# FFN up-projections as 2x2 block products in seven multiplications, with the down-projections in a second phase

## The chip, the core and the metric

One core of a Trainium2 chip runs the program. The time is the device time of one execution in microseconds (us). The engines are PE (TensorE, the matmuls), DVE (VectorE), ACT (ScalarE), POOL (GpSimd) and SP (SyncE, which here only issues DMAs). Each runs its own instructions in order and waits on semaphores for the others.

## The reference

Two layers of a decoder trunk, batch 1, 1024 positions, 1024 channels, all in float32. Layer 0 is a retention layer, layer 1 differential attention over keys and values that are computed once; behind each stands the same kind of FFN, and the FFN is what changes here:

```python
D_FF = 2816                      # 22 blocks of 128
def conv_ffn(xn, w_up, conv_w, conv_b, w_down):
    h = xn @ w_up                # 1024 x 1024 times 1024 x 5632
    hp = jnp.pad(h, ((0, 0), (CONV_WIDTH - 1, 0), (0, 0)))
    hc = conv_b
    for j in range(CONV_WIDTH):  # 3 taps, causal, per channel
        hc = hc + hp[:, j:j + S] * conv_w[j]
    g, u = jnp.split(hc, 2, axis=-1)
    return (jax.nn.silu(g) * u) @ w_down
...
x = x + rms_norm(conv_ffn(rms_norm(x, ffn_norm_pre), ...), ffn_norm_post)
```

## The kernel before

Every large product is made from values split in two: a high part that TensorE takes as it is, and a low part that holds the rest. A product is then three matmuls (`mm3`, L96: high by high, high by low, low by high) that add up in one PSUM bank. The split of an operand (`split_to`, L81) is a copy on ACT for the high part and a subtraction on DVE for the low part.

Weights come through `load_w` (L85): a DMA from SP into one of two raw buffers (`rawp`, 1024 columns each, taken in turn in the order of the program), a multiplication by the norm's gain on POOL where there is one (L90), and the split into one of five `hl` buffers. A raw buffer is free for the next load when the low part is taken.

An FFN is run by `gated` (L479): the 22 blocks of 128 hidden channels go in eleven groups, one of 1, nine of 2 and one of 3. For each block `ffn_up` (L591) makes the gate block f and the up block 22 + f: for either, 2 halves of 512 positions x 8 k-blocks x 3 matmuls of 128x512 (`proj_t`). ACT and DVE run the convolution straight out of PSUM (L600, L604), ACT the Silu, POOL the product of the two (L611), and the split puts it into one of three `act` buffers. `down` (L501) multiplies a finished group by its rows of w_down: for each of 8 blocks of 128 positions, 6 matmuls per hidden block (L492) into one PSUM tile, which DVE adds to an accumulator in SBUF (L508, L510). The down products of group g are issued behind the first up block of group g + 1, so up and down products alternate on PE. PSUM is four tiles of two banks.

The norm ahead of the FFN is done by `finish` (L129), block by block of 128 positions, while PE runs the last products of the stage before: the scaled row block (ACT, L186) is transposed on PE (L120) and split into `xh`/`xl`. The first half of the first two up blocks is issued before the last of these blocks is through.

The order of instructions on an engine is set by the framework's scheduler from the order of the code, except where `manual_schedule` fixes it for named engines.

Of the kernel before, what the change touches and what calls it, by code (L numbers as in the profile page):

```python
# [12 lines left out]
F32 = mybir.dt.float32  # L13
F32R = mybir.dt.float32r
# [7 lines left out]
P = 128  # L22
# [28 lines left out]
def trunk(ctx: ExitStack, tc: tile.TileContext, A, out):  # L51
# [13 lines left out]
    gains4 = const.tile([P, 4, NK], F32, name="gains4")  # L65
# [30 lines left out]
    def mm3(out, sh, sl, mh, ml, start, stop):  # L96
        nc.tensor.matmul(out, sh, mh, start=start, stop=False)  # L97
        nc.tensor.matmul(out, sh, ml, start=False, stop=False)  # L98
        nc.tensor.matmul(out, sl, mh, start=False, stop=stop)  # L99
# [22 lines left out]

    def into_xt(ps, sb, xt):
        xh, xl = xt
        c, b = divmod(sb, 4)
        cols = slice(b * P, (b + 1) * P)
        split_to(xh[c][:, :, cols], xl[c][:, :, cols], ps)

    def finish(mm, add, pool, psp, gpost, x_old, x_new, xt, order=tuple(range(NS)), turn_first=False, late=()):  # L129
# [34 lines left out]
        for t in range(NS + 3):  # L164
# [3 lines left out]
            with tc.manual_schedule(engines=ORDERED):  # L168
# [15 lines left out]
                if c is not None:  # L184
                    xh = live["xh", c] = pool.tile([P, D], F32, name="xhn", tag="w4")
                    nc.scalar.activation(out=xh, in_=live.pop(("t", c)), func=AF.Copy, scale=live.pop(("q", c)))  # L186
# [77 lines left out]
    with ExitStack() as p1:  # L264
# [23 lines left out]
        with tc.tile_pool(name="p0", bufs=3, side="right") as p0:  # L288
# [37 lines left out]
            for i in range(2):  # L326
                nc.sync.dma_start(out=gains4[:, 2 + i, :], in_=A["ffn_norm_pre"][i])
# [151 lines left out]
    def gated(wk, up, n_blk, w_down, fin):  # L479
# [49 lines left out]
        rest = iter(())  # L529
        if isinstance(acts[-1], tuple):  # L530
            acts[-1], rest = acts[-1]
            next(rest)

        def mm(sb):
# [10 lines left out]
            if sb == 1:  # L545
                next(rest, None)
# [44 lines left out]
    def ffn_up(wk, layer, xt, tail, w_pool=None, late=None, on_drained=None):  # L591

        cw = []
        gpre = gains4[:, 2 + layer, :]

        def conv(n, ps, hc, c0, c1):
            if not cw:
                cw.append(wk.gp.tile([P, 2 * NF, 4], F32, name="cw"))
                nc.sync.dma_start(out=cw[0], in_=A["conv"][layer])
            nc.scalar.activation(out=hc[:, c0:c1], in_=ps[:, c0:c1], func=AF.Identity, scale=cw[0][:, n, 2:3],  # L600
                                 bias=cw[0][:, n, 3:4])
            for j in (1, 2):
                b = max(c0, j)
                nc.vector.scalar_tensor_tensor(out=hc[:, b:c1], in0=ps[:, b - j:c1 - j],  # L604
                                               scalar=cw[0][:, n, 2 - j:3 - j],
                                               in1=hc[:, b:c1], op0=ALU.mult, op1=ALU.add)

        def gate(hg, hu, act, c0, c1, eng):
            cs = slice(c0, c1)
            nc.scalar.activation(out=hg[:, cs], in_=hg[:, cs], func=AF.Silu)  # L610
            eng.tensor_tensor(out=hg[:, cs], in0=hg[:, cs], in1=hu[:, cs], op=ALU.mult)  # L611
            split_to(act[:, 0, cs], act[:, 1, cs], hg[:, cs])

        def tiles():
            return [wk.w4.tile([P, S], F32, name="hc", tag="w4") for _ in range(2)]

        def up(f):
            ns = (f, NF + f)
            if f == NF - 1:
                return up_last(ns)  # L620
            pss = []
            if f == 0:
                ws = []

                def load():
                    ws.extend(load_w(w_pool or wk.hlp, A["w_up"][layer, n], gpre) for n in ns)
                if late is None:
                    load()
                else:
                    late.append(load)  # L630
                for u in range(2):
                    next(tail)
                    pss.append(psp.tile([P, S], F32, name="ps"))
                    proj_t(pss[u], ws[u], xt, (0,))
                for _ in tail:
                    pass
                for ps, w in zip(pss, ws):
                    proj_t(ps, w, xt, (1,))
                if on_drained is not None:
                    on_drained()  # L640
            hc = tiles()
            for u, n in enumerate(ns):
                if f > 0:
                    w = load_w(wk.hlp, A["w_up"][layer, n], gpre)
                    pss.append(psp.tile([P, S], F32, name="ps"))
                    proj_t(pss[u], w, xt)
                conv(n, pss[u], hc[u], 0, S)
            act = wk.actp.tile([P, 2, S], F32R, name="act")
            gate(*hc, act, 0, S, nc.gpsimd)
            return act  # L650

        def up_last(ns):

            ws = [load_w(wk.hlp, A["w_up"][layer, n], gpre) for n in ns]
            hc = tiles()
            pss = [psp.tile([P, S], F32, name="ps") for _ in ns]
            for u, n in enumerate(ns):
                proj_t(pss[u], ws[u], xt, (0,))
                conv(n, pss[u], hc[u], 0, 512)
            act = wk.actp.tile([P, 2, S], F32R, name="act")  # L660
            gate(*hc, act, 0, 512, nc.vector)

            def rest():
# [502 lines left out]
```

## Time and profile before

| | us |
|---|---|
| median of 3 runs | 2941.19 (2940.98 to 2942.84) |
| the profiled execution | 2942.96 |
| its span, first to last instruction | 2941.2 |
| PE busy in the span | 2880.3 (98%) |
| DVE, ACT, POOL busy | 1469.9, 946.5, 668.4 |
| layer 0's FFN, about | 888 to 1600 |
| layer 1's FFN, about | 2180 to 2935 |

The page cuts the span into 40 equal slices and gives each engine's busy share in tenths; PEclk is the clock that TensorE was granted, in tenths of full speed. Matmuls overlap in the array, so the length of one matmul is not what it adds to the time: that is the distance from start to start. A row of waits names who waited, for whom, the total, how often and the longest.

### The profile page before, as it was taken

Reading aid. Unit: us, or ns where it says so; the run is one execution under the profiler, and the core shown is the slowest. Engines: PE = TensorE matmul, PEld = TensorE weight load, DVE = VectorE, ACT = ScalarE, POOL = GpSimd, SP = SyncE. Lnnn points to the kernel's source line nnn. Section 1 sums busy time; section 2 is a strip of 40 time slices with the busy share of each in tenths; the row PEclk is TensorE's granted clock in tenths of the full one; section 3 lists DMA queues with packets and bytes.
Section 4 is the critical chain, followed back from the end, with each engine's and each line's share of the span. In section 5 each row is a group of like instructions: output and inputs, shape, how many; then the busy total and the mean of one; then the engine's idle time right before and its main releaser. Section 6 shows DMA issues by size and latency. Waiting matters only on the chain. (4 is left out here: it accounts for less than half of the span.)

```text
span 2941.2 us, 35261 instructions
## 1 busy us (share of the span) xinstructions
PE 2880.3 (98%) x14452; PEld 2436.4 (83%) x14452; DVE 1469.9 (50%) x1722; ACT 946.5 (32%) x1462; POOL 668.4 (23%) x744
## 2 busy tenths in 40 slices
PE   8999999999999999999999999999999999999998
PEld 7898989888877888888888788888777888888886
DVE  4433433434446444444445687777554444444445
ACT  3323222211134222222224565555453222222222
POOL 1111120000033111211114334444332121121113
PEclk9999999999999999999999999999999999999999
DMA  4111111321232111111113332233252111111112
GB/s 141 53 54 51 51 52 37 121 79 59 78 122 86 51 50 43 51 50 51 43 44 120 118 80 75 68 85 93 73 204 80 43 50 51 47 47 44 58 58 100
DMA packets 86225, 210.45 MB, mean 72 GB/s; under 512 B 9648, under 2 KB 35248, under 8 KB 86064
## 3 DMA queue, kind: packets, MB, share of 16 engines
q1 hardware_dynamic: 62432, 180.67, 19.3%
q10 hardware_dynamic: 23632, 27.53, 2.9%
q8 instruction: 114, 1.87, 0.3%
q14 instruction: 47, 0.39, 0.0%
HBM read 164.12 MB, written 31.46 MB: 66 GB/s over the span
## 5 line engine op out<-in xcount | busy, mean ns | idle before, releaser
L97 PE MATMUL ps<-xh,hl 128*128 128x512 f32 x1952 | 764.3, 392 | 3.7 <-DVE xl L83 2.4
L99 PE MATMUL ps<-xh,hl 128*128 128x512 f32 x1952 | 762.3, 391 | 0.0
L98 PE MATMUL ps<-xl,hl 128*128 128x512 f32 x1952 | 760.0, 389 | 0.5 <-DVE xl L83 0.5
L492 PE MATMUL ps<-hl,act 128*128 128x512 f32 x2880 | 664.5, 391 | 1.1 <-DVE acc L508 1.1
L492 PEld LDWEIGHTS ps<-hl,act 128*128 128x128 f32 x2880 | 540.8, 188 | 114.3 <-DVE acc L508 1.9
L604 DVE SCALAR_TENSOR_TENSOR hc<-ps,cw,hc 128x1023 f32<-128x1023 f32 (+4 forms) x184 | 226.6, 1232 | 536.8 <-ACT hc L600 536.5
L90 POOL TENSOR_TENSOR raw<-raw,gains 128x1024 f32<-128x1024 f32 x120 | 238.0, 1984 | 1124.3 <-DMA raw<-in_w_up 1032.7
L99 PEld LDWEIGHTS ps<-xh,hl 128*128 128x128 f32 x1952 | 366.9, 188 | 79.7
L97 PEld LDWEIGHTS ps<-xh,hl 128*128 128x128 f32 x1952 | 367.0, 188 | 79.6 <-DVE xl L83 2.6
L98 PEld LDWEIGHTS ps<-xl,hl 128*128 128x128 f32 x1952 | 366.8, 188 | 78.8 <-DVE xl L83 1.0
L82 ACT ACTIVATE hl<-raw 128x1024 fp32r<-128x1024 f32 x228 | 240.0, 1054 | 500.3 <-PE ps L492 320.0
L83 DVE TENSOR_TENSOR hl<-raw,hl 128x1024 fp32r<-128x1024 f32 x228 | 289.9, 1272 | 114.2 <-ACT hl L82 114.0
L510 DVE TENSOR_TENSOR acc<-ps,acc 128x1024 f32<-128x1024 f32 x192 | 234.6, 1222 | 148.4 <-PE ps L492 147.1
L600 ACT ACTIVATE hc<-ps,cw 128x1024 f32<-128x1024 f32 (+1 forms) x92 | 107.6, 1170 | 485.1 <-PE ps L99 475.7
L611 POOL TENSOR_TENSOR hc<-hc 128x1024 f32<-128x1024 f32 x42 | 100.8, 2400 | 346.8 <-DVE hc L604 319.9
L97 PE MATMUL ps<-hl,xh 128*128 128x256 f32 x544 | 154.9, 286 | 1.7 <-ACT xh L82 1.7
L99 PE MATMUL ps<-hl,xl 128*128 128x256 f32 x544 | 155.3, 286 | 0.8 <-DVE xl L83 0.7
L98 PE MATMUL ps<-hl,xh 128*128 128x256 f32 x544 | 154.8, 285 | 0.0
L853 ACT ACTIVATE s<-s,m 128x256 f32<-128x256 f32 (+7 forms) x128 | 99.1, 775 | 102.1 <-POOL m L852 101.7
L82 ACT ACTIVATE act<-hc 128x1024 fp32r<-128x1024 f32 (+1 forms) x46 | 47.1, 1024 | 239.9 <-POOL hc L611 231.1
L97 PEld LDWEIGHTS ps<-hl,xh 128*128 128x128 f32 x544 | 105.2, 194 | 2.8 <-ACT xh L82 2.6
L99 PEld LDWEIGHTS ps<-hl,xl 128*128 128x128 f32 x544 | 105.3, 194 | 1.6 <-DVE xl L83 1.5
(188 smaller groups left out, 3701.1 us busy)
## 6 DMA issues: line engine op xcount, KB each, us to landing
raw<-in_w_up SPq DMA_DIRECT2D x88, 512.0 KB, 3.5
raw<-in_w_down SPq DMA_DIRECT2D x44, 512.0 KB, 3.5
raw<-in_w_t SPq DMA_DIRECT2D x32, 512.0 KB, 3.5
xold<-x SPq DMA_DIRECT2D x24, 512.0 KB, 4.6
raw<-in_w_v SPq DMA_DIRECT2D x16, 512.0 KB, 3.5
oret<-t ACTq DMA_DIRECT2D x32, 256.0 KB, 2.3
raw<-in_a_w_out SPq DMA_DIRECT2D x16, 512.0 KB, 3.6
on<-oret SPq DMA_DIRECT2D x16, 512.0 KB, 4.6
```

The costliest lines, as they stand in the source:

```text
L82: nc.scalar.activation(out=hi, in_=src, func=AF.Copy)
L83: nc.vector.tensor_tensor(out=lo, in0=src, in1=hi.bitcast(F32), op=ALU.subtract)
L90: nc.gpsimd.tensor_tensor(out=v, in0=v, in1=gain.unsqueeze(2).broadcast_to([P, gain.shape[1], n]), op=ALU.mult)
L97: nc.tensor.matmul(out, sh, mh, start=start, stop=False)
L98: nc.tensor.matmul(out, sh, ml, start=False, stop=False)
L99: nc.tensor.matmul(out, sl, mh, start=False, stop=stop)
L492: nc.tensor.matmul(ps[:, half, :], a, ws[f][:, m, hs], start=f == 0 and n == 0, stop=f == len(ws) - 1 and n == 2)
L510: nc.vector.tensor_tensor(out=acc[sb], in0=flat(ps), in1=acc[sb], op=ALU.add)
L600: nc.scalar.activation(out=hc[:, c0:c1], in_=ps[:, c0:c1], func=AF.Identity, scale=cw[0][:, n, 2:3], bias=cw[0][:, n, 3:4])
L604: nc.vector.scalar_tensor_tensor(out=hc[:, b:c1], in0=ps[:, b - j:c1 - j], scalar=cw[0][:, n, 2 - j:3 - j], in1=hc[:, b:c1], op0=ALU.mult, ...
L611: eng.tensor_tensor(out=hg[:, cs], in0=hg[:, cs], in1=hu[:, cs], op=ALU.mult)
L853: nc.scalar.activation(out=s[:, :w], in_=s[:, :w], func=AF.Exp, scale=0.125, bias=m, accum_out=l[:, c:c + 1])
```

## The change

**The product.** For a pair (gate block f, up block 22 + f) the weights are a 2x2 block matrix, 2 blocks of output channels (gate, up) by 2 halves of K (512 channels each), and the normed input another, 2 halves of K by 2 halves of the positions. The four output blocks are made from seven block products instead of eight (Winograd's form), each of 128 x 512 x 512, that is 4 k-blocks x 3 matmuls of 128x512. The seven operands of the input side are x11, x21 (first half of the positions, as before) and t2, t3, t1, t4, x22, sums and differences of quarters, made once per layer and split; the seven of the weight side are made for each pair: a11, s2, a21', s1, a12, a22, a12', with four additions on POOL and seven splits of 512 columns (`weights`, `split_part`). Five additions on DVE (`plus`) put the four output blocks together out of PSUM, in SBUF. The convolution then reads SBUF.

**The input.** `Staged` takes the place of `new_xt`: the second half of the positions is kept raw, and so is a raw copy of the first. The norm's gain is multiplied into the row block by DVE (one operation with the scaling) in place of POOL's multiplication of every weight. The x11 products of the first four pairs are issued among the last transposes, and their x21 products behind them.

**The phases.** All 22 pairs of a layer run first. Each finished block is written to DRAM (`acts[f]`, by ACT's DMA queue). Then pools are opened for `gated` with `stored` as its up function: it loads a block back through a raw buffer, splits it, and the down products follow with no up products between them. The matmul order in the up loop is fixed by `manual_schedule` on PE. The late half of the last up block (`up_last`, `rest`) is gone.

```diff
+    def ffn_up(layer, xt, tail, w_pool, late, on_drained):
+        N_PRE = 4
+        acts = [dram.tile([P, S], F32, name=f"act{layer}_{f}") for f in range(NF)]
...
+        def prod(out, w, x, onto=False):
+            for k in range(4):
+                ws = slice(k * P, (k + 1) * P)
+                mm3(out, w[0][:, ws], w[1][:, ws], x[0][:, k, :], x[1][:, k, :], not onto and k == 0, k == 3, onto)
...
+        up = st.enter_context(tc.tile_pool(name=f"u{layer}", bufs=7, reuse_waits="tile"))
+        sp = st.enter_context(tc.tile_pool(name=f"s{layer}", bufs=3, reuse_waits="tile"))
+        cp = st.enter_context(tc.tile_pool(name=f"c{layer}", bufs=1, reuse_waits="tile"))
+        ring = st.enter_context(tc.tile_pool(name=f"ring{layer}", bufs=8, reuse_waits="tile"))
...
+        for b in range(4):
...
+            nc.vector.tensor_tensor(out=x11, in0=x12, in1=x11, op=ALU.subtract)
+            nc.vector.tensor_tensor(out=t2, in0=x22, in1=x11, op=ALU.subtract)
+            both("t2", t2, nc.vector)
+            nc.vector.tensor_tensor(out=x12, in0=x22, in1=x12, op=ALU.subtract)
+            both("t3", x12, nc.vector)
+            both("t1", x11, nc.gpsimd)
+            nc.gpsimd.tensor_tensor(out=x21, in0=x21, in1=t2, op=ALU.subtract)
+            both("t4", x21, nc.vector)
+            both("x22", x22, nc.gpsimd)
...
+            nc.gpsimd.tensor_tensor(out=s1, in0=a21, in1=a22, op=ALU.add)
+            nc.gpsimd.tensor_tensor(out=s2, in0=s1, in1=a11, op=ALU.subtract)
+            yield split_part(s2)
...
+            prod(b, next(ws), ops["t2"])
+            u2 = half_tile()
+            plus(u2, b, first.pop(f))
+            step()
+            prod(c, next(ws), ops["t3"])
+            u3 = half_tile()
+            plus(u3, c, u2)
+            step()
+            prod(d, next(ws), ops["t1"])
...
+            nc.scalar.activation(out=cg, in_=cg, func=AF.Silu)
+            nc.gpsimd.tensor_tensor(out=cg, in0=cg, in1=cu, op=ALU.mult)
+            nc.scalar.dma_start(out=acts[f], in_=cg)
...
+    def stored(wk, acts):
+        def up(i):
+            raw = load_raw(acts[i])
             act = wk.actp.tile([P, 2, S], F32R, name="act")
...
+            split_to(act[:, 0, :], act[:, 1, :], raw)
             return act
...
-    tail = gated(wk, ffn_up(wk, 0, xt, tail), NF, rows(A["w_down"][0], NF), last)
...
+    acts = ffn_up(0, xt, tail, wk.hlp, None, drained)
+    open_ops(wk, "f")
+    open_mid(wk, "f", "left")
+    tail = gated(wk, stored(wk, acts), NF, rows(A["w_down"][0], NF), last)
```

**SP's queue, in the FFN loop of layer 0.** Before (raw buffers are numbered in the order in which they are taken; the rows cover two groups of the loop):

```order
L78 DMA raw_7449<-in_w_up 128x1024
L78 DMA raw_7507<-in_w_up 128x1024
L78 DMA raw_7572<-in_w_up 128x1024
L78 DMA raw_7630<-in_w_up 128x1024
L78 DMA raw_7693<-in_w_down 128x1024
L78 DMA raw_7698<-in_w_down 128x1024
L78 DMA raw_7817<-in_w_up 128x1024
L78 DMA raw_7875<-in_w_up 128x1024
```

In the down phase after the change (`act0_4` is stored block 4; blocks 5 and 6 are group 3, the two `in_w_down` behind them are group 2's weights, blocks 3 and 4):

```order
L78 DMA raw_10113<-act0_4_6341 128x1024
L78 DMA raw_10118<-act0_5_6342 128x1024
L78 DMA raw_10123<-in_w_down 128x1024
L78 DMA raw_10128<-in_w_down 128x1024
L78 DMA raw_10245<-act0_6_6343 128x1024
L78 DMA raw_10250<-act0_7_6344 128x1024
L78 DMA raw_10255<-in_w_down 128x1024
L78 DMA raw_10260<-in_w_down 128x1024
```

Stored blocks and down weights now share the two raw buffers, and each weight of a group stands behind a stored block whose split needs an act buffer of the group before.

**POOL at the entry of layer 0's FFN.** Before, residuals of the last row blocks and the gains of the first weights:

```order
L155 TENSOR_TENSOR acc_4585<-acc_4585,xold_6547 128x1024
L90 TENSOR_TENSOR raw_7081<-raw_7081,gains4_76 128x1024
```

After the change, from the last reciprocal roots of the norm on:

```order
L105 TENSOR_TENSOR rstd_6784<-rstd_6784,mhalf_74 128x1
L703 TENSOR_TENSOR xraw0_4375<-xraw0_4375,t2raw_6944 128x4x128
L703 TENSOR_TENSOR xraw0_4375<-xraw0_4375,t2raw_6959 128x4x128
L703 TENSOR_TENSOR xraw0_4375<-xraw0_4375,t2raw_6974 128x4x128
L696 TENSOR_TENSOR t1l_6939<-xraw0_4375,t1h_6938 128x4x128
L696 TENSOR_TENSOR x22l_6943<-xraw1_4376,x22h_6942 128x4x128
L703 TENSOR_TENSOR xraw0_4375<-xraw0_4375,t2raw_6989 128x4x128
L696 TENSOR_TENSOR t1l_6939<-xraw0_4375,t1h_6938 128x4x128
L726 TENSOR_TENSOR s1_7010<-raw_7008 128x512
L696 TENSOR_TENSOR x22l_6943<-xraw1_4376,x22h_6942 128x4x128
L696 TENSOR_TENSOR t1l_6939<-xraw0_4375,t1h_6938 128x4x128
L696 TENSOR_TENSOR x22l_6943<-xraw1_4376,x22h_6942 128x4x128
```

The sums of the input's quarters and the low parts of t1 and x22 now stand on POOL ahead of s2, the operand of the first t2 product, which is the next row. On DVE, 23 operations stand between the last transposes and the low part of s2, among them these:

```order
L696 TENSOR_TENSOR t2l_6935<-t2raw_6974,t2h_6934 128x4x128
L696 TENSOR_TENSOR t3l_6937<-xraw1_4376,t3h_6936 128x4x128
L696 TENSOR_TENSOR t4l_6941<-xraw0_4375,t4h_6940 128x4x128
L696 TENSOR_TENSOR t3l_6937<-xraw1_4376,t3h_6936 128x4x128
L696 TENSOR_TENSOR t2l_6935<-t2raw_6989,t2h_6934 128x4x128
L696 TENSOR_TENSOR t4l_6941<-xraw0_4375,t4h_6940 128x4x128
L673 TENSOR_TENSOR wc_7014<-s2_7011,wc_7014 128x512
```

**DVE where the down products begin, layer 0.** Before, copies of the first down group among convolutions and splits of the next up blocks:

```order
L604 SCALAR_TENSOR_TENSOR hc_6880<-ps_6945,cw_6866,hc_6880 128x1023
L508 COPY acc_7014<-ps_7007 128x1024
L83 TENSOR_TENSOR hl_7265<-raw_7262,hl_7265 128x1024
L508 COPY acc_7023<-ps_7016 128x1024
L604 SCALAR_TENSOR_TENSOR hc_6880<-ps_6945,cw_6866,hc_6880 128x1022
L508 COPY acc_7032<-ps_7025 128x1024
```

After the change, from the last addition of the up loop on (`act_9896` is stored block 0, `hl_9906` the first down weight):

```order
L747 TENSOR_TENSOR hbuf1_7005<-ps_9768,u_9795 128x512
L83 TENSOR_TENSOR act_9896<-raw_9894,act_9896 128x1024
L83 TENSOR_TENSOR act_9901<-raw_9899,act_9901 128x1024
L742 SCALAR_TENSOR_TENSOR hbuf0_7004<-hbuf1_7005,cw_6858,hbuf0_7004 128x1023
L742 SCALAR_TENSOR_TENSOR hbuf0_7004<-hbuf1_7005,cw_6858,hbuf0_7004 128x1022
L83 TENSOR_TENSOR hl_9906<-raw_9904,hl_9906 128x1024
L83 TENSOR_TENSOR act_9983<-raw_9981,act_9983 128x1024
L529 COPY acc_9916<-ps_9909 128x1024
L529 COPY acc_9925<-ps_9918 128x1024
L83 TENSOR_TENSOR hl_9993<-raw_9991,hl_9993 128x1024
```

The first stored block's split now stands behind the last addition of the up loop, and the first down weight behind that split.

## Rows read from the trace of the kernel before

**Rows 1.** The page: busy us (share of the span) xinstructions; granted clock in tenths

```profile
PE 2880.3 (98%) x14452; PEld 2436.4 (83%) x14452; DVE 1469.9 (50%) x1722; ACT 946.5 (32%) x1462; POOL 668.4 (23%) x744
...
PEclk9999999999999999999999999999999999999999
```

**Rows 2.** Windows in both FFN loops: us, busy us by engine, clock, DMA share, GB/s

```profile
960.00:1560.00 600.00, 600.00 (x2649) 497.01 (x2648) 267.72 (x219) 138.11 (x129) 111.11 (x54) 1.00 0.16 49
2280.00:2880.00 600.00, 600.00 (x2629) 493.36 (x2628) 267.75 (x219) 136.99 (x128) 108.78 (x54) 1.00 0.16 49
```

**Rows 3.** Waits of PE from 910 to 1600 us: total, times, longest

```profile
PE ps L97 <- ACT xh L82: 1.1, 1, 1.1
PE ps L492 <- DVE acc L508: 0.6, 1, 0.6
```

**Rows 4.** Timeline of PE from 840 to 915 us, rows with idle time: start, us

```profile
864.85 1.97 PE L120 MATMUL ps<-ident,xhn 128*128 128x128 f32 x8 [3.70 <-ACT xhn L186]
...
895.57 1.09 PE L120 MATMUL ps<-ident,xhn 128*128 128x128 f32 x8 [1.58 <-ACT xhn L186]
...
904.99 3.44 PE L120 MATMUL ps<-ident,xhn 128*128 128x128 f32 x16 [2.85 <-ACT xhn L186]
909.54 0.96 PE L97 MATMUL ps<-xh,hl 128*128 128x512 f32 x3 [1.11 <-ACT xh L82]
```

**Rows 5.** Windows behind two of these gaps, columns as in rows 2

```profile
865.00:870.00 5.00, 5.00 (x16) 4.27 (x17) 3.26 (x3) 3.21 (x4) 4.39 (x6) 0.50 0.54 196
870.00:875.00 5.00, 5.00 (x26) 4.18 (x25) 1.88 (x3) 3.67 (x6) 3.85 (x6) 0.95 0.55 162
...
905.00:910.00 5.00, 3.89 (x18) 3.61 (x19) 1.71 (x2) 3.03 (x3) 1.90 (x1) 0.70 0.16 65
```

**Rows 6.** Instruction groups by form: count, busy us, mean ns of one, idle before

```profile
L97 PEld LDWEIGHTS ps<-xh,hl 128*128 128x128 f32 x1952 | 367.0, 188 | 79.6 <-DVE xl L83 2.6 <-ACT xh L82 1.4 <-ACT hl L82 0.6
...
L83 DVE TENSOR_TENSOR hl<-raw,hl 128x1024 fp32r<-128x1024 f32 x228 | 289.9, 1272 | 114.2 <-ACT hl L82 114.0
L82 ACT ACTIVATE hl<-raw 128x1024 fp32r<-128x1024 f32 x228 | 240.0, 1054 | 500.3 <-PE ps L492 320.0 <-PE ps L99 149.9 <-PE pj L99 13.0
...
L604 DVE SCALAR_TENSOR_TENSOR hc<-ps,cw,hc 128x1023 f32<-128x1023 f32 x84 | 107.8, 1283 | 523.4 <-ACT hc L600 523.4
...
L600 ACT ACTIVATE hc<-ps,cw 128x1024 f32<-128x1024 f32 x84 | 101.4, 1207 | 464.9 <-PE ps L99 455.5 <-DMA cw<-in_conv 9.4
L611 POOL TENSOR_TENSOR hc<-hc 128x1024 f32<-128x1024 f32 x42 | 100.8, 2400 | 346.8 <-DVE hc L604 319.9 <-ACT hc L610 15.8 <-issue 11.2
...
L610 ACT ACTIVATE hc<-hc 128x1024 f32<-128x1024 f32 x42 | 44.5, 1060 | 110.1 <-DVE hc L604 110.0
...
L83 DVE TENSOR_TENSOR atl<-pst,ath 128x512 fp32r<-128x512 f32 x48 | 32.6, 682 | 2.3 <-ACT ath L82 2.2
...
L82 ACT ACTIVATE ath<-pst 128x512 fp32r<-128x512 f32 x48 | 28.0, 586 | 4.2 <-PE pst L870 4.1
L508 DVE COPY acc<-ps 128x1024 f32<-128x1024 f32 x24 | 28.0, 1213 | 0.0
```

**Rows 7.** Timeline of DVE in the retention's rotary step: start us, us, instruction

```profile
71.58 0.68 DVE L345 TENSOR_TENSOR t<-ps,sin 128x512 f32<-128x512 f32 x1
72.18 0.67 DVE L83 TENSOR_TENSOR qk0l<-t,qk0h 128x512 fp32r<-128x512 f32 x1
72.78 0.68 DVE L344 TENSOR_TENSOR t<-ps,sin 128x512 f32<-128x512 f32 x1
73.38 1.17 DVE L83 TENSOR_TENSOR qk0l<-t,qk0h 128x512 fp32r<-128x512 f32 x1
```

**Rows 8.** One POOL line: least, median and longest ns, first and last start

```profile
L346 POOL TENSOR_TENSOR t<-t,t x32: 1290/1452/1667, 68.0 to 443.3; 128x512 f32<-128x512 f32 x32
```

**Rows 9.** Timeline of POOL in the stretch of rows 7

```profile
72.34 1.67 POOL L346 TENSOR_TENSOR t<-t,t 128x512 f32<-128x512 f32 x1 [1.76 <-DVE t L345]
```

**Rows 10.** Loads of w_down: least, median and longest us from issue to landing

```profile
DMA to landing us min/median/max: 3.3/3.5/4.8
```

More of the change, by code (lines that the diff above doesn't have):

```diff
@@ L64, in trunk @@
     nc.vector.memset(mhalf, -0.5)
-    gains4 = const.tile([P, 4, NK], F32, name="gains4")
+    gains4 = const.tile([P, 2, NK], F32, name="gains4")
     junk = [None]
@@ L94, in load_w, with mm3 @@
         return hl
[L96 to L99, printed above, removed]
+    def mm3(out, sh, sl, mh, ml, start, stop, onto=False):
+        nc.tensor.matmul(out, sh, mh, start=start, stop=False, skip_group_check=onto)
+        nc.tensor.matmul(out, sh, ml, start=False, stop=False, skip_group_check=onto)
+        nc.tensor.matmul(out, sl, mh, start=False, stop=stop, skip_group_check=onto)
     def rstd(ss, eps):
@@ L121, in transposed, with __init__, put @@
         return ps
+    class Staged:
+        def __init__(self, pool, gain):
+            self.gain = gain
+            self.h, self.l = (pool.tile([P, NK, 512], F32R, name=f"x{n}0", tag=f"x{n}0") for n in "hl")
+            self.raw = [pool.tile([P, NK, 512], F32, name=f"xraw{c}", tag=("xh1", "xl1")[c]) for c in range(2)]
+            self.pool = pool
+        def put(self, ps, c, cols):
+            if c == 0:
+                split_to(self.h[:, :, cols], self.l[:, :, cols], ps)
+            nc.scalar.activation(out=self.raw[c][:, :, cols], in_=ps, func=AF.Copy)
     def into_xt(ps, sb, xt):
-        xh, xl = xt
         c, b = divmod(sb, 4)
         cols = slice(b * P, (b + 1) * P)
+        if isinstance(xt, Staged):
+            xt.put(ps, c, cols)
+            return
+        xh, xl = xt
         split_to(xh[c][:, :, cols], xl[c][:, :, cols], ps)
@@ L185, in finish @@
                     xh = live["xh", c] = pool.tile([P, D], F32, name="xhn", tag="w4")
-                    nc.scalar.activation(out=xh, in_=live.pop(("t", c)), func=AF.Copy, scale=live.pop(("q", c)))
+                    if isinstance(xt, Staged):
+                        nc.vector.scalar_tensor_tensor(out=xh, in0=live.pop(("t", c)), scalar=live.pop(("q", c)),
+                                                       in1=xt.gain, op0=ALU.mult, op1=ALU.mult)
+                    else:
+                        nc.scalar.activation(out=xh, in_=live.pop(("t", c)), func=AF.Copy, scale=live.pop(("q", c)))
                 if a is not None:
@@ L589, in ret_up @@
         return up
[L591 to L601, printed above, removed]
-            for j in (1, 2):
[L603 to L647, printed above, removed]
@@ L648, in up @@
+    def stored(wk, acts):
+        def up(i):
+            raw = load_raw(acts[i])
             act = wk.actp.tile([P, 2, S], F32R, name="act")
-            gate(*hc, act, 0, S, nc.gpsimd)
+            split_to(act[:, 0, :], act[:, 1, :], raw)
             return act
[L652 to L663, printed above, removed]
-                for u, n in enumerate(ns):
-                    proj_t(pss[u], ws[u], xt, (1,))
-                    conv(n, pss[u], hc[u], 512, S)
-                    if u == 1:
-                        gate(*hc, act, 512, S, nc.vector)
-                    yield
-            return act, rest()
@@ L1089, in last @@
         return finish(mm, add, wk.w4, psp, g, x3, x_out, None)
-    tail = gated(wk, ffn_up(wk, 1, xt, tail, o5, late, drained), NF, rows(A["w_down"][1], NF), last)
+    acts = ffn_up(1, xt, tail, o5, late, drained)
+    open_ops(wk, "b")
+    open_mid(wk, "b", "right")
+    tail = gated(wk, stored(wk, acts), NF, rows(A["w_down"][1], NF), last)
     for _ in tail:
```

160 lines of the change are left out of this document (142 added, 18 removed).

## The prediction

> **What bounds the kernel now.** I read the page first: TensorE (PE) is busy for 98% of the span, at the full clock but for a few dips [rows 1]. A busy share does not price a matmul, so the second view is two stretches of 600 us inside the two FFN loops [rows 2]: PE is never idle there and runs 2649 and 2629 matmuls, one per 0.2265 and 0.2282 us. The 0.39 us of a single matmul row is its pipelined length; the pace is the price. VectorE (DVE) is busy for 45% of those stretches and GpSimd (POOL) for 18%. Third, the waits of layer 0's whole FFN: 1.7 us [rows 3]. So an FFN now costs its matmuls, because up- and down-projections alternate and one covers the loads and splits of the other. What an uncovered wait costs is seen where the FFN is entered: gaps of 3.70, 1.58, 2.85 and 1.11 us [rows 4], and behind the long ones a granted clock at the lower of its two levels, 1.2 instead of 2.4 GHz: 0.50 and 0.95 in the two stretches of 5 us behind the gap of 3.70 us, 0.70 in the one that holds most of what follows the gap of 2.85 us [rows 5]. That is 5 x 0.50 + 5 x 0.05 = 2.75 us of work lost after one and 5 x 0.30 = 1.5 us after the other.
>
> The profiled execution took 2942.96 us, its span 2941.2; the median of the runs is 2941.19. I add to 2941.2, which is the median.
>
> **Matmuls removed.** A pair of blocks (gate f, up f) took 2 weights x 2 halves x 8 k-blocks x 3 = 96 matmuls and takes 7 x 4 x 3 = 84. 12 x 22 pairs x 2 layers = 528; the built programs hold 14452 and 13924, so that the change might not do what it says is no rival here. At the pace of rows 2: 264 x 0.2265 + 264 x 0.2282 = **-120 us**. The shapes stay, and a weight load (0.188 us [rows 6]) still fits under the pace.
>
> **The up loop, blocks 4 to 21.** PE needs 84 x 0.2273 = 19.1 us. Per block DVE has seven splits and five additions of 512 columns and four convolution passes: 12 x 0.68 + 4 x 1.28 us by [rows 6], a little less back to back (starts 0.60 apart in [rows 7]), so 12 to 13.3 us. POOL has four additions of 512 (1.29 to 1.67 us, [rows 8]; I take the shortest, since the longer ones hold a wait for DVE) and the gate product (2.40): 7.6 to 8. ScalarE (ACT) has nine passes of 512 (0.59) and three of 1024 (1.21, 1.21, 1.06): 9. Each fits, but DVE and POOL exclude each other: the subtraction at 73.38 us, both of whose operands are in SBUF, takes 1.17 instead of 0.67 us, as it waits until POOL's operation (72.34 to 74.01) ends; beside the same POOL operation a product that reads PSUM (72.78) takes its usual 0.68 [rows 7, 9]. Fully serial this is 12 + 8 = 20 us; the five additions read PSUM (3 us) and can run beside POOL, which leaves 17, under 19.1. PE reuses a bank two products (5.4 us) after the one whose sum must be out of it. I take 0, and (20 - 19.1) x 36 = 32 us as the upper bound; a gain is excluded, the matmuls being counted.
>
> **Blocks 0 to 3** have five products (13.6 us), and the same POOL and convolution work: 10 x 0.60 + 4 x 1.2 = 10.8 on DVE plus 8 on POOL less 3 that overlap = 15.8. That is 2.2 us too long four times, **+8 per layer**; bounds 0 (PE's slack swallows it) and 4 x (18.8 - 13.6) = 21.
>
> **The FFN's entry.** The products t2 to x22 need sums of all four quarters of x. In the order printed ahead, between the last transposes and the first t2 product DVE has 23 operations of 512 on SBUF operands and POOL 12, the last of which makes s2. The lock makes them serial: 1.1 (copy out of PSUM) + 23 x 0.60 + 12 x 1.29 = 30.4 us. PE's cover is the three X21 products ahead of t2, 36 x 0.2265 = 8.2. The gap is 22.2, against 1.1 now [rows 4]; extra operations ahead of the last normalisation add about 1, the deeper clock dip about 1: **+23 per layer**. Without the lock POOL's chain alone is 1.1 + 12 x 1.29 + 1.2 for the split = 17.8, gap 9.6, +10; with POOL at its slowest (1.67) it is +28.
>
> **Start of the down phase.** In DVE's order the split of the first stored block stands behind the last addition of the up loop; the first down weight uses the buffer which that split frees. The load is then 0.7 + 1.27 + 3.5 [rows 10] + 1.05 = 6.5 us behind PE's last product. In ACT's queue that weight's split also stands behind the last block's convolution and Silu: 0.7 + 1.21 + 1.27 (another split on DVE) + 2 x 1.28 + 1.06 + 1.05 = 7.9. With about 0.1 us a handover, PE waits some 8.2 us. The first group has one block (6 x 8 matmuls, 10.9 us) and DVE eight copies of 1.21 plus four splits, which stand between the copies and each wait for a load: another 2.5 us. With a dip of 2.75: **+13 per layer**; bounds 7 (load path, mild dip) and 17.
>
> **Group boundaries of the down phase.** Raw buffers are two, taken in program order; the second activation block of group g+1 takes its buffer before the first weight of g+1. Three act buffers hold two blocks of g and one of g+1. So at each boundary: PE's last use of group g's first act is 6 matmuls, 1.36 us, before its last matmul; then ACT splits the new act (1.05), DVE takes the low part (1.27), only then SP can issue the weight's load (3.5 [rows 10]), ACT splits it (1.05), and PE starts. -1.36 + 1.05 + 1.27 + 3.5 + 1.05 = 5.5 us, with a few handovers of some 0.1 us each **5.8 us of idle PE**. Nothing covers it: the group is 96 matmuls, all down products, and the next group's all need that weight. Now the same two raw buffers turn round behind the 192 up matmuls (43 us) that stand between two down groups, without a wait [rows 3]. The clock: gaps of 2.85 and 3.70 cost 1.5 and 2.75 us [rows 4, 5]; I take 2.1, their middle. 7.9 us x 9 boundaries (from group 1 to group 10) x 2 layers = **+142**. Bounds: 5.1 (landing of 3.3, no handovers) + 1.2 = 6.3, so 113; 5.8 + 2.75 + 0.3 = 8.9, so 160.
>
> The rows show that the alternation is what keeps PE fed. The Trainium skill says so too, against this change: "Perfetto Trace Analysis", Optimization Strategy, advises interleaving the regimes of a kernel whose most-contended engine changes. By that alone the split into two phases would have a cost, without a figure; the sum is from the rows.
>
> **Sum:** -120 + 16 + 46 + 26 + 142 = +110; 2941 + 110 = **3051 us**.
>
> **The rivals.** (a) *The loads arrive in time at the boundaries.* For it: DMA is lightly used, 0.16 in the loops [rows 2], and loads of the same size never made PE wait there [rows 3]. Against: the order ties each load to a split that waits for PE. Priced without the boundaries: 2941 - 120 + 16 + 46 + 26 = 2909, faster. It decides from 32/18 = 1.8 us a boundary downward; a landing alone takes 3.3 [rows 10]. (b) *Only the count of matmuls matters:* PE is the engine that is full [rows 1, 2], so 120 us come off: 2821. The Trainium skill's "Perfetto Trace Analysis", Identifying the Most-Contended Engine, has the engine with the highest occupancy optimized first, which is this reading. Against it stand the gaps of rows 4, which appear wherever cover is missing. (c) *The lock is mild:* DVE and POOL overlap at the entries and in blocks 0 to 3, but the boundaries stay: 3051 - 26 - 16 = 3009. (d) *The lock binds the whole up loop:* DVE, in order, also waits for ACT and PE; at 2 us a block over 36 blocks, 3051 + 72 = 3123.
>
> **How the numbers follow.** Forecast 0.65, (c) 0.16, (d) 0.09, (a) 0.06, (b) 0.02, and 0.02 for a sum of small errors that ends within 0.2% of now (about what a measurement of this kernel can tell from no change). Slower is 0.65 + 0.16 + 0.09 = 0.90, same 0.02, faster 0.08. The range reaches down to (c) with boundaries at 6.6 us, 3009 - 24 = 2985, and up to the forecast with the upper bounds of the boundaries (+18) and the entries (+10) and part of those of the loop (+16 of 32) and the first blocks (+10 of 26): 3105. (a), (b) and most of (d) lie outside, 0.17.
>
> **What would show it.** In the profile after: the waits of PE should name the split of a down weight some 18 times at 5 to 6 us each, and its windows in the down phases show PE idle for a fifth and the clock under 1.0; a gap of some 20 us ahead of the first t2 product in each layer, with DVE and POOL busy by turns; up-loop windows of blocks 4 to 21 with PE at 100% and 84 matmuls per 19.1 us. No waits at the boundaries, or a landing well under 3.3 us, would make the prediction wrong downward; PE gaps inside blocks 4 to 21 upward.

## The result and the profile after

The changed kernel takes 3388.38 us (3384.89 to 3392.09, four runs) against 2941.62 us of the kernel before beside it: 1.152 times as long, 95% interval 1.150 to 1.154. The profiled execution has a span of 3386.4 us. The forecast was 3051 us, 2985 to 3105: slower, as it turned out, but 447 us slower instead of 110.

The page of the changed kernel, against [rows 1]: busy us (share of the span) and instructions by engine; the costliest groups that wait, with busy us, mean ns and the idle time ahead of them; the granted clock in tenths:

```profile
PE 2930.2 (87%) x13924; PEld 2415.6 (71%) x13924; DVE 1896.5 (56%) x2200; ACT 1106.2 (33%) x1790; POOL 826.4 (24%) x858
...
PEclk9999999999889898998898999999989999898998
...
L513 PE MATMUL ps<-hl,act 128*128 128x512 f32 x2880 | 711.4, 410 | 125.5 <-ACT hl L82 123.7
...
L98 PE MATMUL ps<-t1h,wc 128*128 128x512 f32 x176 | 97.0, 551 | 148.6 <-DVE u L747 148.6
```

PE has 528 matmuls less and is idle for 13% of a longer span. Two groups carry most of that: the first matmul of a down group waits for the high part of its weight (123.7 us, the boundaries and the two starts of the down phase that the forecast had), and the first matmul of the product t1 waits for an addition of DVE (148.6 us), which the forecast did not have.

The windows of the up loop and of the down phase of layer 0, to set beside [rows 2] (us; busy us by engine with instructions: PE, weight loads, DVE, ACT, POOL; clock; DMA share; GB/s):

```profile
1060.00:1500.00 440.00, 353.35 (x1357) 273.53 (x1358) 262.98 (x257) 141.52 (x193) 136.66 (x79) 0.91 0.16 58
1560.00:1820.00 260.00, 210.06 (x827) 169.30 (x826) 125.21 (x105) 40.21 (x38) 4.00 (x2) 0.89 0.23 75
```

Both phases look alike: PE idle for a fifth of the time and the clock at 0.9. That was expected of the second one alone; idle PE in blocks 4 to 21 is the sign that the forecast had named for being wrong upward. In the first a matmul now takes 440 / 1357 = 0.324 us where [rows 2] had 0.2265, which is 27 us for a block of 84 instead of 19.1.

PE's waits while blocks 4 to 21 of layer 0 run (total us, times, longest), to set beside the 1.7 us of [rows 3]:

```profile
PE ps L98 <- DVE u L747: 69.4, 19, 4.7
PE ps L98 <- DVE hbuf L747: 15.9, 20, 0.9
PE ps L98 <- ACT u L668: 12.4, 18, 0.7
```

One block of this loop in the timeline, a few rows of each engine (start us, us, instruction, in brackets the idle time before it and its releaser):

```profile
1299.52 0.50 PE L98 MATMUL ps<-x22h,wc 128*128 128x512 f32 x1 [0.78 <-DVE hbuf L747]
...
1305.95 0.50 PE L98 MATMUL ps<-t2h,wc 128*128 128x512 f32 x1 [0.69 <-ACT u L668]
...
1310.66 0.68 DVE L747 TENSOR_TENSOR u<-ps,u 128x512 f32<-128x512 f32 x1
...
1311.79 0.61 ACT L672 ACTIVATE wc<-raw 128x512 fp32r<-128x512 f32 x1
1311.96 2.34 POOL L802 TENSOR_TENSOR hbuf<-hbuf 128x1024 f32<-128x1024 f32 x1 [2.97 <-ACT hbuf L801]
...
1312.44 2.41 DVE L673 TENSOR_TENSOR wc<-raw,wc 128x512 fp32r<-128x512 f32 x1 [1.10 <-ACT wc L672]
...
1314.77 0.68 DVE L747 TENSOR_TENSOR u<-ps,u 128x512 f32<-128x512 f32 x1
...
1315.51 0.50 PE L98 MATMUL ps<-t1h,wc 128*128 128x512 f32 x1 [3.81 <-DVE u L747]
```

Read it backwards. The product d (t1) starts at 1315.51, when the second addition `u` (1314.77, `plus(u3, c, u2)`) has ended. That addition reads the bank of c; d writes the other bank of the same two-bank tile `cd`, and needs nothing of the sum. In DVE's order the addition stands behind a low part (1312.44) that takes 2.41 us while POOL's gate product (1311.96 to 1314.30) runs beside it, and that low part itself waited for ACT. (Without the gate product it takes 0.69 us, as an experiment below shows.) The same happens on a smaller scale at t2 (waits for ACT's copy of a, its neighbour in `pq`) and at x22 (waits for the addition that reads c). By the releasers in these rows the framework puts the wait on the tile, not on the bank.

### The profile page after: what moved, and what is told of

Read it like the earlier page. It is cut to its first block, busy times and chain, and to the rows that moved or that the text cites. A ratio compares the mean times of both kernels' runs of the same rounds, so it can differ in the third digit from the quotient of the medians.

```text
span 3386.4 us, 35697 instructions
## 1 busy us (share of the span) xinstructions
PE 2930.2 (87%) x13924; PEld 2415.6 (71%) x13924; DVE 1896.5 (56%) x2200; ACT 1106.2 (33%) x1790; POOL 826.4 (24%) x858
## 5 line engine op out<-in xcount | busy, mean ns | idle before, releaser
L513 PE MATMUL ps<-hl,act 128*128 128x512 f32 x2880 | 711.4, 410 | 125.5 <-ACT hl L82 123.7
L673 DVE TENSOR_TENSOR wc<-raw,wc 128x512 fp32r<-128x512 f32 x212 | 228.3, 1080 | 128.7 <-ACT wc L672 127.3
L83 DVE TENSOR_TENSOR hl<-raw,hl 128x1024 fp32r<-128x1024 f32 x144 | 184.9, 1285 | 170.2 <-ACT hl L82 170.1
L672 ACT ACTIVATE wc<-raw 128x512 fp32r<-128x512 f32 x212 | 132.1, 626 | 402.2 <-PE ps L100 393.5
L98 PE MATMUL ps<-xh,hl 128*128 128x512 f32 x576 | 225.5, 392 | 2.6 <-DVE xl L83 2.4
L98 PE MATMUL ps<-t1h,wc 128*128 128x512 f32 x176 | 97.0, 551 | 148.6 <-DVE u L747 148.6
L99 PE MATMUL ps<-xl,hl 128*128 128x512 f32 x576 | 224.5, 390 | 0.3 <-DVE xl L83 0.3
L100 PE MATMUL ps<-xh,hl 128*128 128x512 f32 x576 | 224.4, 390 | 0.0
L747 DVE TENSOR_TENSOR hbuf<-ps,u 128x512 f32<-128x512 f32 x132 | 90.9, 689 | 220.4 <-PE ps L100 220.4
L742 DVE SCALAR_TENSOR_TENSOR hbuf<-hbuf,cw,hbuf 128x1023 f32<-128x1023 f32 (+1 forms) x132 | 188.7, 1429 | 32.6 <-ACT hbuf L740 31.4
L90 POOL TENSOR_TENSOR raw<-raw,gains 128x1024 f32<-128x1024 f32 x32 | 68.3, 2136 | 335.2 <-DMA raw<-in_w_kv_k 294.6
L98 PE MATMUL ps<-xh,wc 128*128 128x512 f32 x320 | 132.2, 413 | 15.5 <-ACT u L668 8.0
L726 POOL TENSOR_TENSOR s<-raw 128x512 f32<-128x512 f32 x44 | 61.9, 1407 | 303.9 <-DMA raw<-in_w_up 296.1
```

The costliest lines, as they stand in the source:

```text
L83: nc.vector.tensor_tensor(out=lo, in0=src, in1=hi.bitcast(F32), op=ALU.subtract)
L90: nc.gpsimd.tensor_tensor(out=v, in0=v, in1=gain.unsqueeze(2).broadcast_to([P, gain.shape[1], n]), op=ALU.mult)
L98: nc.tensor.matmul(out, sh, mh, start=start, stop=False, skip_group_check=onto)
L99: nc.tensor.matmul(out, sh, ml, start=False, stop=False, skip_group_check=onto)
L100: nc.tensor.matmul(out, sl, mh, start=False, stop=stop, skip_group_check=onto)
L513: nc.tensor.matmul(ps[:, half, :], a, ws[f][:, m, hs], start=f == 0 and n == 0, stop=f == len(ws) - 1 and n == 2)
```

## The experiments

Where no number of runs is given, a time is that of one run. The nine runs of one of these kernels lie up to 9 us apart, so a difference of that size is not clear by itself.

**Own tiles.** Each product gets a tile of its own, out of the same four of the pool:

```diff
-            pq = psp.tile([P, 2, 512], F32, name="ps")
-            cd = psp.tile([P, 2, 512], F32, name="ps")
+            def bank():
+                return psp.tile([P, 2, 512], F32, name="ps")[:, 0, :]
             if full:
-                a, b = pq[:, 0, :], pq[:, 1, :]
+                a, b = bank(), bank()
...
-            c, d = cd[:, 0, :], cd[:, 1, :]
+            c, d = bank(), bank()
```

> Each of the four products a, b, c, d gets a PSUM tile of its own instead of half of a two-bank tile; the number of tiles in the pool stays four. Theory 1 (shared tiles): in the changed kernel PE may not write one bank of a tile before the other bank has been read, so t2 waits for the copy of a, and t1 for the addition u3 of c, right behind the product that they follow. Then PE's wait at t1 (69 us in the 22 blocks of layer 0) goes, as do those at t2 and x22, and the distance from t2 to t2 falls from 27.1 us to 19.5 to 21; 36 blocks x 6 to 7.5 us = 220 to 270 us less, 3115 to 3170 us. Theory 2 (the lock of DVE and POOL binds the loop): DVE is busy for 16.5 us of a block, POOL for 8.6, and one after the other they fill 25 us; the wait moves to another product, the distance stays over 25 us, and the time over 3310 us.

3118.4 us, 270 less. PE's waits in blocks 4 to 21 of layer 0, and a window of the loop:

```profile
PE ps L98 <- DVE u L747: 1.2, 5, 0.3
```

```profile
1060.00:1360.00 300.00, 297.96 (x1289) 239.70 (x1288) 270.94 (x245) 129.27 (x182) 140.63 (x75) 1.00 0.24 82
```

From t2 to t2 it is now, in layer 0, 19.0 us in the first of these blocks and 19.5 to 19.8 in the later ones. DVE is busy for 90% of the window and POOL for 47%, a good part of it each waiting for the other, and it costs PE next to nothing. So the mutual exclusion does not bind the loop; the shared tiles did. (DVE's order changes a little with the edit, since the scheduler sets it; the waits that go are those named above.)

**The distance.** Two-bank tiles as in the changed kernel, but a and c share one and b and d the other, and x22 comes ahead of t4, so that one product lies between a product and the next one in its tile:

```diff
-                a, b = pq[:, 0, :], pq[:, 1, :]
+                a, b = pq[:, 0, :], cd[:, 0, :]
-            c, d = cd[:, 0, :], cd[:, 1, :]
+            c, d = pq[:, 1, :], cd[:, 1, :]
...
+            w4 = next(ws)
+            prod(d, next(ws), ops["x22"], True)
+            hg = h_first.pop(f)
+            plus(hg[:, 512:], d, u2)
+            step()
+            prod(c, w4, ops["t4"])
+            plus(hu[:, :512], c, u3)
```

> The changed kernel with its two two-bank tiles per block as before, but a and c share one and b and d the other, and the last two products change places (x22 ahead of t4). Each product then follows, with one product of 2.7 us between, the one whose reader must have been there. Theory 1 (what costs is the distance between a product and the next one in the same tile): at distance nothing the wait at t1 was 3.7 us, at t2 0.7, at x22 0.9, and the block 27 us; with 2.7 us between, about 1 us at the product behind u3 stays and the others go: 20 to 21.5 us a block, 3388 - 36 x 6 = 3130 to 3190 us, a little over the 3118 us of own tiles. Theory 2 (two banks of a tile in use at once cost by themselves, or the number of tiles counts): still 25 us or more a block, over 3300 us.

3180.1 us, 21.1 us a block (in a few 22.9). PE's waits in these blocks of layer 0:

```profile
PE ps L98 <- DVE u L747: 29.5, 17, 2.0
```

The wait left over stands at t1, for the addition that reads b, one product back; about 1 us was expected, at the product behind u3. With no product between, a block of layer 0 takes 27.1 us, with one 21.1, with two (own tiles) 19.0 to 19.8. Of the 2.1 us over 19.0 this wait is 1.7, so two banks of one tile in use at once cost little, if anything, by themselves; the distance does.

**The lock under shared tiles, and without them.** POOL's gate product is left out, once from the changed kernel, once from the one with own tiles:

```diff
             nc.scalar.activation(out=cg, in_=cg, func=AF.Silu)
-            nc.gpsimd.tensor_tensor(out=cg, in0=cg, in1=cu, op=ALU.mult)
             nc.scalar.dma_start(out=acts[f], in_=cg)
```

> The changed kernel without POOL's product of gate and up block (so the stored blocks are the gate alone): 2.34 us of POOL per block are gone, everything else stays. Theory 1 (shared tiles): PE still waits for u3 at every t1, but u3 stands behind a low part that itself stood behind the gate product; the wait falls from 3.7 to about 2 us a block, 36 x 1.7 to 2.3 us = 60 to 85 less, 3300 to 3330 us, and the wait at t1 remains the largest. Theory 2 (the lock fills the block): a block loses all of 2.34 us and the waits for the other POOL operations remain, 3300 us, but then the distance follows the sum of DVE and POOL work. The two are told apart by the first experiment, this one prices the lock under the shared tiles.

> Own tiles (3118.4 us) without POOL's product of gate and up block, the stored blocks being the gate alone. With shared tiles this operation cost 97.5 us, 2.7 per block. If it cost that only because every late addition stopped PE at the next product, it now costs little: the loop runs at PE's pace, with 2 us of idle PE in 18 blocks, and at most the 0.6 us by which the later blocks are longer than the first ones (19.6 and 19.0) goes: 3095 to 3118 us. If the lock costs a block its time by itself, the saving is again 2 us or more a block, under 3050 us.

With shared tiles 3290.9 us, 97.5 less, somewhat more than expected. The waits of blocks 4 to 21, a window, and on DVE the low part that stands ahead of the addition `u3`:

```profile
PE ps L98 <- DVE u L747: 38.8, 18, 3.0
PE ps L98 <- DVE hbuf L747: 14.1, 18, 0.8
```

```profile
1060.00:1440.00 380.00, 321.13 (x1336) 249.98 (x1334) 233.24 (x254) 139.47 (x190) 97.92 (x62) 0.99 0.20 67
```

```profile
1113.24 0.69 DVE L673 TENSOR_TENSOR wc<-raw,wc 128x512 fp32r<-128x512 f32 x1 [1.10 <-ACT wc L672]
```

The low part takes 0.69 us in place of 2.41, so POOL's product did hold it up. The wait at t1 falls from 3.7 to some 2.2 us and stays the largest one; and the granted clock goes from 0.91 to 0.99. That is why a block loses more than the 1.5 us of wait: 3.3 in these windows (27.2 and 23.9 us for 84 matmuls), 97.5 / 36 = 2.7 over the whole. With own tiles it is 3090.0 us, 28.4 less, 5 below what was expected:

```profile
1060.00:1360.00 300.00, 300.00 (x1326) 248.39 (x1325) 240.54 (x248) 135.97 (x184) 111.13 (x60) 1.00 0.24 83
```

PE is never idle and a block of layer 0 is 19.0 us, the 84 matmuls. The same POOL instruction costs 97.5 us where the next product stands behind a DVE addition, and 28.4 where it has two products of room.

**Four act buffers.** In both FFNs, for one `hl` buffer less:

```diff
-        wk.hlp = st.enter_context(tc.tile_pool(name="hlp" + tag, bufs=5, reuse_waits="tile"))
-        wk.actp = st.enter_context(tc.tile_pool(name="act" + tag, bufs=3, reuse_waits="tile"))
+        wk.hlp = st.enter_context(tc.tile_pool(name="hlp" + tag, bufs=5 if tag == "a" else 4, reuse_waits="tile"))
+        wk.actp = st.enter_context(tc.tile_pool(name="act" + tag, bufs=3 if tag == "a" else 4, reuse_waits="tile"))
```

> In both FFNs four act buffers instead of three, and four hl buffers instead of five (the room is the same). Theory 1 (the forecast's mechanism at the boundaries): a stored block's split no longer waits for PE, so the raw buffer comes free and the first weight of the next group is there in time; of PE's waits at the down products (62 us in layer 0 with the first one of 12) only the first one of each layer and the last boundary (its group of three wants three weights beside two in use) stay. 16 boundaries x (5.6 us of wait and about 2.2 of clock) = 125 less, 3250 to 3275 us. Theory 2 (the transfers themselves are too slow for two raw buffers): four loads of 3.5 us, each with a split of 1.27 behind it, turn round in two buffers in about 10 us of a group's 22, so this would not show; if it did, the waits would only halve: 3320 to 3340 us.

3245.4 us, 143 less. The first two views are of the changed kernel: PE's waits for weights in layer 0's down phase, and one boundary in the timeline. The third is the clock behind that gap (columns as in [rows 2]). With four buffers, the fourth has the waits of layer 0's down phase, the fifth those for weights in the whole run, the sixth a window of the phase:

```profile
PE ps L513 <- ACT hl L82: 61.9, 10, 11.9
```

```profile
1591.28 1.06 ACT L82 ACTIVATE act<-raw 128x1024 fp32r<-128x1024 f32 x1 [20.72 <-PE ps L513]
...
1592.37 1.23 DVE L83 TENSOR_TENSOR act<-raw,act 128x1024 fp32r<-128x1024 f32 x1 [1.23 <-ACT act L82]
...
1593.63 2.60 SPq L78 DMA_DIRECT2D raw<-in_w_down  x2
...
1597.04 1.06 ACT L82 ACTIVATE hl<-raw 128x1024 fp32r<-128x1024 f32 x1 [3.35 <-DMA raw<-in_w_down]
...
1598.15 4.21 PE L513 MATMUL ps<-hl,act 128*128 128x512 f32 x9 [5.55 <-ACT hl L82]
```

```profile
1598.00:1603.00 5.00, 4.85 (x11) 3.84 (x12) 2.45 (x2) 1.16 (x2) 0.00 (x0) 0.50 0.51 171
1603.00:1608.00 5.00, 5.00 (x22) 4.10 (x21) 0.00 (x0) 0.00 (x0) 0.00 (x0) 0.92 0.23 94
```

```profile
PE ps L121 <- ACT xhn L209: 10.1, 2, 9.9
PE ps L513 <- DVE acc L529: 1.4, 2, 1.0
```

```profile
PE ps L513 <- ACT hl L82: 23.2, 2, 12.0
```

```profile
1560.00:1740.00 180.00, 180.00 (x796) 149.05 (x795) 117.38 (x100) 36.02 (x34) 0.00 (x0) 1.00 0.30 97
```

The boundary is the chain of the forecast, link by link: the act split released by PE, the low part, the load, the weight's high part, a gap of 5.55 us and a clock of 0.50 behind it. In layer 0 nine boundaries and the start of the phase make the 61.9 us. With one act buffer more all 18 are gone, the last ones too (expected to stay), at the same two raw buffers and the same transfers; what still waits for a weight are the two starts (23.2 us).

**Both.** 

> Both edits together, own PSUM tiles and four act buffers. They act in different phases, so by theory 1 their gains add up: 3388 - 245 - 125 = about 3020 us, 2970 to 3060. By theory 2 of either one: 3180 to 3260 us.

2966.7 us, a little under the sum of the two (3388 - 270 - 143 = 2975). What now eats up the saved matmuls is at the entries, in blocks 0 to 3, and where the down phases begin and layer 0's ends.

**Early first load of the down phase.** The memory of t2, t3, t1 and t4 becomes that of the act and hl buffers, and in the last block, behind c, the first stored block and the first weight are loaded and split:

```diff
+        wk.actp = Turn(cp, ("t2h", "t2l", "t3h", "t3l"))
+        wk.hlp = Turn(cp, ("t1h", "t1l", "t4h", "t4l"))
...
             plus(u3, c, u2)
             step()
+            if f == NF - 1:
+                wk.first = stored(wk, acts)(0), load_w(wk.hlp, rows(A["w_down"][layer], NF)[0])
```

> On top of own tiles and four act buffers (2966.7 us): the first stored block and the first down weight are loaded and split inside the last block of the up loop, into the memory of the operands t2, t3 (act) and t1, t4 (weights), which stay allocated as the buffers of the down phase. Theory 1: the 12 us in which PE stands at the first down product (11.9 and 12.6 us in the run with both edits) come only from the split of the stored block standing behind the last addition of the up loop, and the load behind that split; then they go but for 0 to 2 us, with the clock dip behind them (about 2.5): 2 x 13 = 26 less, 2935 to 2945 us. Theory 2: the additional splits in the last block delay the block's own additions and the first copies of the down phase, which then come last: half of it stays, 2950 to 2958 us.

2944.1 us, 22.6 less. The 11.9 and 12.6 us at the first down products are gone; waits of PE for DVE's first copies of the accumulators come in their place, 1.2 and 1.6 us in layer 0 and 4.5 in layer 1.

**The entry on DVE.** The four sums and eight low parts that POOL made go to DVE, and t2 is made for all columns first:

```diff
-            both("t1", x11, nc.gpsimd)
-            nc.gpsimd.tensor_tensor(out=x21, in0=x21, in1=t2, op=ALU.subtract)
...
-            both("x22", x22, nc.gpsimd)
...
+            nc.vector.tensor_tensor(out=x21, in0=x21, in1=t2, op=ALU.subtract)
...
+        for n, q in (("t1", 1), ("t4", 2), ("x22", 4)):
+            for b in range(4):
+                both(n, quarters(b)[0], quarters(b)[q])
```

> On top of own tiles and four act buffers (2966.7 us): at the entry all sums and low parts of the input's operands are DVE's (POOL keeps the weights' sums), and t2 is made for all four columns before t3, t1, t4 and x22. Theory 1 (the lock makes DVE and POOL one engine at the entry, so what counts is the sum of their work ahead of the first t2 product): between 931 and 950 us of that run every DVE and every POOL operation takes some 1.7 us, each waiting for the other; some ten operations go from 1.29 to 0.60 us, 7 us, and up to 16 low parts no longer stand ahead of t2, so the gaps ahead of the first t2 products and inside them shrink: 7 to 14 us a layer, 2938 to 2953 us. Theory 2 (POOL's and DVE's chains run beside each other, and ACT's 20 high parts ahead of the copy of a finished bank set the gap): under 5 us a layer or a loss, since DVE gets more to do: 2957 to 2975 us.

2959.0 us, 7.7 less: this lies in the second theory's range, though the difference is no larger than runs of one kernel can differ. The lock is there all the same. In the run with both edits, behind the last transposes of layer 0, a window and four rows of DVE (the second word of a row is its length):

```profile
931.00:950.00 19.00, 11.50 (x33) 8.40 (x34) 19.00 (x13) 7.40 (x14) 18.50 (x11) 0.68 0.05 19
```

```profile
931.32 0.68 DVE L696 TENSOR_TENSOR t2l<-t2raw,t2h 128x512 fp32r<-128x512 f32 x1
931.92 1.76 DVE L696 TENSOR_TENSOR t3l<-xraw,t3h 128x512 fp32r<-128x512 f32 x1
933.60 1.77 DVE L696 TENSOR_TENSOR t4l<-xraw,t4h 128x512 fp32r<-128x512 f32 x1
935.30 1.76 DVE L696 TENSOR_TENSOR t2l<-t2raw,t2h 128x512 fp32r<-128x512 f32 x1
```

For 19 us DVE and POOL count as busy almost without a break and take turns: a low part of 0.68 us takes 1.76, as one POOL operation goes between. The Trainium skill has this as an exclusive lock ("SBUF — State Buffer", SBUF: two separate sides): of a DVE operation with two inputs in SBUF and a GpSimd operation that reads SBUF, whichever starts first holds the shared ports for its whole length, and the other is blocked. The rows agree. Freeing POOL did not help as much as that would have it. One thing that came last instead is seen: in the run of this edit the third X21 product still waits 5.91 us for ACT's copy of its bank, which stands behind the operands' high parts in ACT's order.

**All four edits.** 

> Own tiles, four act buffers, early first down load and the entry on DVE together. By theory 1 of both: 2966.7 - 26 - 21 = 2920 us, 2908 to 2935, faster than the kernel before by 0.2 to 1.1%. By theory 2 of both: 2945 to 2965, not faster.

2933.8 us (2928.6 to 2937.8, nine runs), ratio 0.9975, interval 0.9965 to 0.9985: 0.25% shorter than the kernel before, at the slow end of what was expected.

**And the gate product on DVE.**

```diff
-            nc.gpsimd.tensor_tensor(out=cg, in0=cg, in1=cu, op=ALU.mult)
+            nc.vector.tensor_tensor(out=cg, in0=cg, in1=cu, op=ALU.mult)
```

> The kernel with all four edits (2933.8 us), with the product of gate and up block moved from POOL to DVE. Theory 1 (what makes the later blocks 19.6 instead of 19.0 us is that DVE waits for POOL's product of 2.34 us): DVE gets an operation of about 1.27 us in place of a wait of up to 2.3, the blocks go to 19.0 to 19.2, 28 blocks x 0.5 = 14 us less: 2915 to 2925 us, faster than the kernel before by 0.6 to 0.9%. Theory 2 (the work on DVE itself makes its additions late, 12 x 0.60 + 4 x 1.25 = 12.2 us and now 13.5): the same time or up to 10 us more, 2930 to 2945 us.

2916.4 us (2914.7 to 2917.6, five runs), ratio 0.9915, interval 0.9902 to 0.9929, as the first theory had it. A window of its up loop:

```profile
1060.00:1340.00 280.00, 280.00 (x1237) 231.94 (x1236) 249.18 (x251) 129.19 (x177) 105.22 (x59) 1.00 0.24 82
```

PE has no idle time there and the full clock. Of the 120 us of matmuls that the change saves, 25 arrive; the rest goes into the entries, blocks 0 to 3 and the end of layer 0's down phase.

## Why the forecast was right and wrong

**Matmuls, -120: right.** In the last window 280 / 1237 = 0.226 us each, and 19.0 us a block.

**Up loop, 0: wrong, and the main error.** From the first matmul of block 4 to the last of block 21 it took 486.1 and 480.8 us where 18 x 19.08 = 343.4 were forecast, 280 us too much. The step that failed is the sentence that PE reuses a bank two products (5.4 us) after the one whose sum must be out of it, and the 0 us that was taken from it. That is so for banks. The waits go by tiles, and there the distance was nothing: a and b, c and d stand in one tile and follow each other. So the addition's whole way through DVE's queue stood on PE's path, and whatever made DVE late (the gate product above all) was paid by PE, with a clock dip on top. The forecast did not ask which tile each wait guards. The bound for the lock, 0 to 32 us, was right for the case it was made for: with own tiles the loop takes 351.1 and 353.3 us, 17 over PE's time.

**The rivals.** (d), the lock binding the whole loop, was the nearest in time (3123) and names the right place, but own tiles leave the lock in and take the loss away. It made a wait longer that another cause had put there. (a) and (b) are out by the boundaries, (c) by the entries, which cost more than it allows and where DVE and POOL take turns.

**Blocks 0 to 3, +16: too small.** From the first t2 to block 4 it took 84.6 and 79.1 us against 4 x 13.6 for the products: +55. With own tiles 75.9 and 72.5, so some 15 of it is the tiles again. The other 40 are put down to the work of DVE and POOL, for which the serial sum per block (2.2 us too long four times is 8.8 a layer, not 8) was too short; that part is not split further.

**Entry, +46: near in sum, by luck, and wrong in place.** The waits of PE at layer 0's entry, and windows of both entries (columns as in [rows 2]):

```profile
868.75 1.94 PE L121 MATMUL ps<-ident,xhn 128*128 128x128 f32 x8 [5.87 <-DVE xhn L206]
...
884.55 1.97 PE L121 MATMUL ps<-ident,xhn 128*128 128x128 f32 x8 [3.24 <-DVE xhn L206]
...
920.37 1.94 PE L121 MATMUL ps<-ident,xhn 128*128 128x128 f32 x8 [6.07 <-DVE xhn L206]
...
935.33 0.80 PE L98 MATMUL ps<-xh,wc 128*128 128x512 f32 x1 [6.11 <-ACT u L668]
...
945.06 0.79 PE L98 MATMUL ps<-t2h,wc 128*128 128x512 f32 x1 [2.66 <-ACT wc L672]
```

```profile
840.00:945.00 105.00, 76.31 (x325) 60.79 (x323) 79.79 (x60) 47.39 (x75) 58.25 (x52) 0.85 0.26 96
2400.00:2483.00 83.00, 64.60 (x281) 50.97 (x280) 57.59 (x57) 44.75 (x70) 39.37 (x38) 0.84 0.33 116
```

Not one gap of 22 us ahead of the first t2 product but several of 2 to 6, from the norm on (compare [rows 4]): DVE's scaling and sums delay the transposes, and ACT's high parts the copy of a finished bank. In these windows PE is idle for 28.7 and 18.4 us, and the lower clock costs about 9 in each while PE is busy: 38 and 27 us. Before, the gaps of [rows 4] and the dips of [rows 5] cost 13.5 in layer 0, and four short gaps cost 3.5 in layer 1. That is +48. The one long gap of the forecast is not there, and waits that it did not have make up for it.

**Start of the down phase, +26: right in sum.** 23 by the early load. The wait itself was longer than the 8.2 us worked out (11.9 and 11.6), and there was less of the rest that was added for copies and the clock.

**Boundaries, +142: right,** 143 by the experiment (152 with own tiles in place), 7.9 us each, by the mechanism that was written down: 5.6 us of wait where 5.8 were worked out.

**Not priced:** at the end of layer 0's down phase PE waits 10.2 us for a normalised row block. The first line is of the changed kernel, the second the longest such wait of the kernel before:

```profile
1836.27 1.97 PE L121 MATMUL ps<-ident,xhn 128*128 128x128 f32 x8 [10.20 <-ACT xhn L209]
```

```profile
1632.68 1.09 PE L120 MATMUL ps<-ident,xhn 128*128 128x128 f32 x8 [1.53 <-ACT xhn L186]
```

All such waits there come to 12.1 us, against 4.4 before: +8. The late half of the last up block, which the change removes, was issued around these blocks before. The removal was seen and not costed. That this half was the cover is argued from its place and was not tried.

Together -120 + 280 + 55 + 48 + 23 + 143 + 8 = 437 of 447 us; 10 are not assigned. The parts come from different runs, and one part's size changes by some 9 us with the edits that are in place beside it (270 or 279 for own tiles, 143 or 152 for the act buffer).

## What to carry to other kernels

When a product is said to have slack before it reuses memory, count the distance in the unit on which the framework puts its waits, here the whole tile, and look in the built order for what each first matmul waits on. Neighbouring products belong in different tiles. Here, with two products between a product and the next one in its tile, the additions that had cost PE 3.7 us a block at t1 cost 1.2 us in 18 blocks. A phase that loses its alternating partner may need one buffer more than it had; here each of its group boundaries showed the whole load chain without it.

## What the runs showed of the hardware

Gaps and the clock. In the up-loop windows above PE is idle for 5.3 us of a block in the changed kernel (86.65 us over 440 / 27.1 = 16.2 blocks) and for 3.7 us without the gate product (58.87 over 16), and busy for 0.260 and 0.240 us a matmul, against 0.226 where there are no gaps; 84 matmuls make that 21.9, 20.2 and 19.0 us. The granted clock is 0.91, 0.99 and 1.00, a mean of stretches at the lower of the two levels (1.2 GHz) and at the upper one (2.4). The clock accounts for the difference of the first two paces (0.226 / 0.91 and 0.226 / 0.99 are 0.248 and 0.228); the 0.012 us that each has over that is the same with either clock. So a gate product of 2.34 us took some 1.7 us of gaps and as much again of PE's pace, more than its own length. Behind the 5.55 us at a boundary the clock is at the lower level (0.50) for the 5 us shown, and at 0.92 in the next 5.

And the Trainium skill's remark on a gap that repeats ("Perfetto Trace Analysis", Optimization Strategy), that there may not be enough PSUM for the next tile, is half the matter here: the gap went with the same four buffers, used one product each.
